# Layer 1's first weights beside layer 0's output, in buffers of their own, and projections ahead of the last output tile

## The chip, the core and the metric

The kernel runs on one core of a Trainium2 chip. The core has five engines that run their own instruction streams and wait for one another through semaphores: TensorE (PE in the profile, PEld for its weight loads), VectorE (DVE), ScalarE (ACT), GpSimd (POOL) and SyncE (SP), which issues most of the transfers between the main memory and the on-chip memory (SBUF). Matmul results go to eight PSUM banks. The metric is the device time of one execution in microseconds (us), lower being better.

## The reference, cut to what matters

Two layers over 1024 latent tokens and 256 context tokens, all in fp32, width 1024. Layer 0 is multi-head latent attention with 16 heads, layer 1 differential attention with 8 heads:

```python
for i in range(2):
    shift, scale, gate = adaln(c, ada_w[i], ada_b[i])           # the context has its own from c_ctx
    h = x * (1.0 + scale[:, None, :]) + shift[:, None, :]
    h_c = ctx * (1.0 + scale_c) + shift_c
    if i == 0: o, o_c = mla_mixer(h, h_c, ...)                  # ends with  o * silu(gate projection)
    else:      o, o_c = diff_mixer(h, h_c, ...)                 # q, k, v, gate = h @ w_in;  o1 - lam_full * o2
    x = layer_norm(DEEPNORM_ALPHA * x + gate[:, None, :] * (o @ out_w[i]), ln_g[i], ln_b[i])
    if i == 0:
        ctx = layer_norm(DEEPNORM_ALPHA * ctx + gate_c * (o_c @ out_w[i]), ln_g[i], ln_b[i])
```

The end of layer 0 is the line with `layer_norm`; its result, scaled and shifted, is the `h` from which layer 1 makes q, k and v. `lam_full` comes from 256 numbers, `diff_lambda`.

## The kernel before, in words

**Precision.** An fp32 matrix product is made of two halves: each operand is split into a high part and a low part (`split`, L175 to L177, for products in a reduced fp32; `split16`, L181 and L182, for fp16 with a scale), and `mm3` (L184 to L187) adds three matmuls: high by high, high by low, low by high. A split is a copy on ScalarE (the high part) and a subtraction on VectorE or GpSimd (the low part).

**Layer 0's output (L853 to L926).** The heads of layer 0 leave their results in `o_d` in main memory. When the last head is done, ten tiles of 128 tokens follow, the two context tiles first (t = 8, 9, 0, 1, ..., 7). Ahead of the first one, two gate rows are loaded. `out_tile` loads a tile of `o_d` and of the gate's silu (`sg_d`), multiplies them on GpSimd (L860), transposes the product on TensorE in two halves (L866, bank "c"), and splits it into `tH` (ScalarE, L176) and `tL` (VectorE, L177). Then TensorE multiplies by the output weights, held in SBUF, in two halves of 512 columns (banks "a" and "b", 24 matmuls each; the records of the three are L185, L186, L187). VectorE evicts each half with the gate and the residual (L877, L878) and takes its statistics (L879, L881); GpSimd raises to the power (L159, L160) and VectorE normalises to `z` (L883). From `z` come two things: the residual of layer 1, written to `zn_d` (VectorE L911, GpSimd L912, a store), and, through eight transposes (L918, bank "d"), layer 1's input `hb` (VectorE L920, GpSimd L922), split into fp16 `h1H` (ScalarE, L925) and `h1L` (GpSimd, L926). The order of instructions on every engine is that of a scheduler in this stage.

**Layer 1's start.** `prod_w(h, which)` makes the weights of one head, `which` being 0 for q and k together and 1 for v and the gate: two loads of 512 KB (L975), a sum of squares on ScalarE (L979), a sum over partitions by a small matmul (L982), an exact power of two as scale (VectorE, GpSimd; L984 to L995, L284 to L287), and two splits into fp16 (L181 on ScalarE, L182 on VectorE). `prod_w(0, 0)` is called behind the tile loop, with its loads on ScalarE's queue and its sum in bank "c". Then the eight PSUM banks become one ring "b" (`set_banks`), the rotary tables and lambda are loaded and lambda computed (L1011 to L1023). `prod_k1`, `prod_q1` and `prod_v1` make K, Q and V of a head. K is made in three chunks (tokens 0 to 511, 512 to 1023, and the 256 of the context), Q in two, each chunk by `proj1` with 24 matmuls, then a rotation (`rope1`, VectorE and GpSimd) and a split whose halves small transfers put in place (`fin`). `prod_w(0, 1)` is woven between K and Q of head 0, `prod_w(1, 0)` between the parts of V. TensorE's order in layer 1 is the order of the text (`manual_schedule`); the other engines' order is the scheduler's.

**Layer 1's gate row** (`gate_row1`, L1208 to L1221) is a vector times matrix made by VectorE with eight loads of 512 KB into the "ws" buffers; its memset, its first load and its first products can be scheduled early, as far as buffers and waits permit.

**Layer 1's output.** During the last head (h = 7), `out_open` closes the pool of the projections and opens one for the output: the rows of `ln_g` and `ln_b`, the buffers `o`, `g`, `tH`, `tL`, `z`, `res`, and the loads and products of out_w's remaining rows (`out_w1`, L1227 and L1229), which the last head's attention runs beside.

**Buffers.** A pool is a stretch of SBUF; `rot` takes the next buffer of a tag from it. A pool opened where an earlier one was closed gives buffers that wait until their memory's earlier user is done. In the kernel before, the pools "a1" and "a1proj" of layer 1 open behind the tile loop, over the memory of the output stage's pool "o0".

Of the kernel before, what the change touches and what calls it, by code (L numbers as in the profile page):

```python
# [9 lines left out]
F32 = mybir.dt.float32  # L10
F32R = mybir.dt.float32r
# [42 lines left out]
def hybrid_kernel(  # L54
# [830 lines left out]

    with ow_ctx, spool("o0") as op0:
# [14 lines left out]
        for t in (8, 9, 0, 1, 2, 3, 4, 5, 6, 7):  # L901
# [12 lines left out]
            hb = op0.tile([P, KT, P], F32, tag="hb", bufs=1, name=nm("hb"))  # L914
            for hh in range(2):
                tb = bank("d")
# [9 lines left out]
            pool.tensor_tensor(h1L[:, :, ts], hb, h1H[:, :, ts], op=ALU.subtract)  # L926

# [3 lines left out]
    TAG1 = {"p0": ([P, NTOK], F32, 2), "p1": ([P, NTOK], F32, 1), "ph": ([P, NT, P], F16, 2),  # L931
# [4 lines left out]
            "ss": ([P, 2], F32, 2), "us": ([P, 1], F32, 3), "es": ([P, 1], F32, 3), "p2s": ([P, 2], F32, 2)}  # L936

    TAGP = {"ws": ([P, 4, 256], F32, 3), "wL": ([P, 4, 256], F16, 4), "wH": ([P, 4, 256], F16, 4),
            "wsq": ([P, D], F32, 1), "sq": ([P, 2], F32, 2), "uw": ([P, 2], F32, 4), "kH": ([P, NTOK], F16, 1), "kL": ([P, NTOK], F16, 1), "gg": ([P, SEQ // P, P], F32, 1),
            "rsw": ([P, 512], F32, 1), "rr": ([P, 512], F32, 1),  # L940
            "kr": ([P, NTOK], F32, 1),
            "Vf": ([P, NT, P], F32, 1), "cosB": ([P, SEQ], F32, 1),
            "sinB": ([P, SEQ], F32, 1)}

    TAGO = {"gb2": ([P, D], F32, 1), "gb3": ([P, D], F32, 1), "o": ([P, D], F32, 3),
            "g": ([P, D], F32, 2), "res": ([P, D], F32, 2), "tH": ([P, KT, P], F32R, 2),
            "tL": ([P, KT, P], F32R, 2), "z": ([P, D], F32, 2), "bs": ([P, 2, 6], F32, 2), "mv": ([P, 4], F32, 2)}
    for k_, v_ in TAG1.items():
        rot(wl, v_[0], v_[1], k_, v_[2], first=True)
# [4 lines left out]
    place = {**{k_: wl for k_ in TAG1}, **{k_: wp for k_ in TAGP}}  # L954
    TAG1.update(TAGP)

    def w1(tag):
        sh, d, b = TAG1[tag]
        return rot(place[tag], sh, d, tag, b)
# [6 lines left out]
    wt, un, us1, es1 = {}, {}, {}, {}  # L966

    def prod_w(h, which, bank_=lambda: bank("b"), load=sp):


        wt[which] = []
        ws, sq = [], w1("sq")
        for q in range(2):
            ws.append(w1("ws"))
            load.dma_start(ws[q], dw[q * 512:(q + 1) * 512, h, which * 256:(which + 1) * 256].rearrange(  # L975
                "(k p) c -> p k c", p=P))
        yield 0
        for q in range(2):
            act.activation(w1("wsq"), ws[q].rearrange("p a b -> p (a b)"), AF.Square, accum_out=sq[:, q:q + 1])  # L979
        yield 0  # L980
        bk = bank_()
        pe.matmul(bk[:, :2], ones, sq, start=True, stop=True)  # L982
        u, p2 = w1("uw"), w1("uw")
        dve.tensor_reduce(u[:, 0:1], bk[:, :2], axis=AX.X, op=ALU.add)  # L984
        pool.tensor_scalar(u[:, 0:1], u[:, 0:1], 1.01, 1e-30, op0=ALU.mult, op1=ALU.add)
        pool.tensor_tensor(u[:, 0:1], u[:, 0:1], poshalf, op=ALU.pow)
        pow2_of(u[:, 1:2], u[:, 0:1], u[:, 0:1], 16384.0, p2)

        dve.tensor_tensor(u[:, 0:1], u[:, 0:1], hun, op=ALU.mult)
        if which:  # L990
            us1[h] = w1("us")
            pool.tensor_tensor(us1[h], u[:, 0:1], vic, op=ALU.mult)
        else:
            es1[h] = w1("es")
            dve.tensor_scalar(es1[h], u[:, 0:1], u[:, 0:1], hic, op0=ALU.mult, op1=ALU.mult)  # L995
        un[which] = u[:, 0:1]
        yield 0
        for q in range(2):
            wH, wL = w1("wH"), w1("wL")
            split16(wH, wL, ws[q], u[:, 1:2])  # L1000
            wt[which] += [(wH[:, j, :], wL[:, j, :]) for j in range(4)]
            yield 0

    for _ in prod_w(0, 0, lambda: bank("c"), act):
        pass
    set_banks(b=8)

    sp.dma_start(cosB, cs1[0])
    sp.dma_start(sinB, cs1[1])
    lamt = w1("rr")[:, :4 * HD]  # L1010
    sp.dma_start(lamt, lam.to_broadcast([P, 4 * HD]))  # L1011
    lt = w1("o1").rearrange("p (a b) -> p a b", a=2)
    ls = w1("sm")
    for j in range(2):
        dve.tensor_tensor(lt[:, j, :], lamt[:, 2 * j * HD:(2 * j + 1) * HD],
                          lamt[:, (2 * j + 1) * HD:(2 * j + 2) * HD], op=ALU.mult)
    dve.tensor_reduce(ls[:, 0:2], lt, axis=AX.X, op=ALU.add)
    act.activation(ls[:, 2:4], ls[:, 0:2], AF.Exp)
    dve.tensor_tensor(nlam, ls[:, 3:4], ls[:, 2:3], op=ALU.subtract)
    dve.tensor_scalar_add(nlam, nlam, -LAMBDA_INIT)  # L1020

    dve.tensor_reduce(lcf[:, 2:3], nlam, axis=AX.X, op=ALU.max, apply_absolute_value=True)
    dve.tensor_scalar_max(lcf[:, 2:3], lcf[:, 2:3], 1.0)  # L1023
    pow2_of(lcf[:, 0:1], lcf[:, 1:2], lcf[:, 2:3], PW, w1("p2s"))
    dve.tensor_tensor(vic, kci, lcf[:, 1:2], op=ALU.mult)

# [455 lines left out]
```

## Time and profile before

| what | us |
| --- | --- |
| median of three runs | 1860.38 |
| lowest and highest run | 1852.12, 1868.84 |
| span of the profiled execution, its own time | 1870.0 |

| stretch of the profiled execution | from | to |
| --- | --- | --- |
| layer 0 up to its last head | 0 | 805 |
| loads of the output stage, until the first transpose | 805.9 | 818.1 |
| ten output tiles on TensorE | 818.1 | 969.4 |
| from the last output matmul to the second K projection | 969.4 | 990.5 |
| layer 1 up to the end | 990.5 | 1870.0 |

The start of a tile is TensorE's first transpose of it (L866): 818.10, 832.78, 846.61, 860.48, 874.63, 894.07, 907.92, 925.73, 939.60, 955.36 for t = 8, 9, 0, ..., 7. In a row of the timeline stand the start, the duration, the engine, the line, the operation and output <- input; in square brackets the idle time ahead of it and what ended it. "xN" means that N instructions in a row are shown as one. A line number is that of the kernel before.

### The profile page before, as it was taken

How to read it: one execution, taken by the hardware profiler on the slowest of the kernel's cores; microseconds unless marked ns; L12 is line 12 of the kernel's file. 1: busy time of each engine (PE TensorE's matmuls, PEld its weight loads, DVE VectorE, ACT ScalarE, POOL GpSimd, SP SyncE). 2: the span in 40 equal slices, each digit the busy share in tenths (PEclk: the TensorE clock that was granted, in tenths of full speed). 3: DMA queues.
4: the chain of work that ended last, by engine and by line, in shares of the span. 5: the costliest groups of instructions: out<-in, count | busy, mean ns of one | idle time of the engine just before them, and what ended most of it. 6: DMA issues, size and time to landing. Idle time of an engine off the chain costs nothing. (4 is left out here: it accounts for less than half of the span.)

```text
span 1870.0 us, 36547 instructions
## 1 busy us (share of the span) xinstructions
PE 1696.2 (91%) x14468; PEld 1237.0 (66%) x14468; DVE 1245.6 (67%) x2072; ACT 1077.1 (58%) x2143; POOL 835.2 (45%) x741
## 2 busy tenths in 40 slices
PE   7889998999999998868979999999999999988998
PEld 3888965656666565556756576767666666666776
DVE  7546766565565657526764777787877777878674
ACT  3432047867777787711123667676767676767542
POOL 1443026767767676646662213222222222433654
PEclk9999799999999999979999999999999999999999
DMA  8245630111111113043333222222121212224341
GB/s 307 62 126 182 189 108 18 39 33 36 42 44 32 32 41 100 25 164 123 124 127 106 71 63 66 62 64 58 56 49 44 59 46 61 63 53 139 99 131 68
DMA packets 111225, 154.84 MB, mean 83 GB/s; under 512 B 13415, under 2 KB 84679, under 8 KB 111054
## 3 DMA queue, kind: packets, MB, share of 16 engines
q1 hardware_dynamic: 104238, 146.22, 26.1%
q10 hardware_dynamic: 6816, 6.29, 1.0%
q8 instruction: 114, 1.87, 0.4%
q14 instruction: 57, 0.47, 0.1%
HBM read 98.65 MB, written 27.07 MB: 67 GB/s over the span
## 5 line engine op out<-in xcount | busy, mean ns | idle before, releaser
L716 POOL TENSOR_TENSOR pl<-p,ph 128x1024 f16<-128x1024 f32 (+1 forms) x176 | 362.8, 2066 | 155.9 <-ACT ph L715 129.5
L1167 ACT ACTIVATE p<-ps_b,mx 128x512 f32<-128x512 f32 (+1 forms) x384 | 230.6, 618 | 83.1 <-DVE mx L1163 82.7
L696 DVE TENSOR_REDUCE mx<-ps_a 128x1 f32<-128x1024 f32 x128 | 155.6, 1223 | 138.2 <-PE ps_a L694 138.2
L714 ACT ACTIVATE p<-ps_a,esc 128x1024 f32<-128x1024 f32 (+1 forms) x176 | 189.2, 1075 | 100.4 <-PE ps_a L772 94.5
L715 ACT CAST ph<-p 128x1024 f16<-128x1024 f32 (+1 forms) x176 | 177.1, 1006 | 5.5
L1161 DVE TENSOR_REDUCE mx<-ps_b 128x1 f32<-128x512 f32 x256 | 165.6, 682 | 0.0
L785 PE MATMUL ps_d<-Vh,pl 128*128 128x65 f16 x1344 | 147.5, 195 | 5.2 <-POOL pl L716 5.1
L782 PE MATMUL ps_d<-Vh,ph 128*128 128x65 f16 x1344 | 149.5, 196 | 0.0
L784 PE MATMUL ps_d<-Vl,ph 128*128 128x64 f16 x1344 | 148.3, 193 | 0.0
L185 PE MATMUL ps_b<-h1H,wH 128*128 128x512 f16 (+1 forms) x384 | 133.5, 348 | 14.1 <-DVE pl L182 6.7
L185 PE MATMUL ps_b<-wH,h1H 128*128 128x256 f16 x512 | 139.5, 272 | 4.4 <-ACT p L1167 4.2
L1192 POOL TENSOR_TENSOR sm<-sm,us 128x1 f32<-128x1 f32 x64 | 18.3, 285 | 271.9 <-DVE sm L1171 258.6
L187 PE MATMUL ps_b<-wH,h1L 128*128 128x256 f16 x512 | 139.5, 273 | 0.0
L186 PE MATMUL ps_b<-wL,h1H 128*128 128x256 f16 x512 | 139.5, 272 | 0.0
L1144 PE MATMUL ps_b<-KS,QS 128*128 128x512 f16 (+1 forms) x384 | 126.1, 345 | 12.0 <-DVE pl L182 6.1
L782 PEld LDWEIGHTS <-ph 128*128 128x128 f16 x1344 | 124.2, 98 | 18.4 <-issue 5.5
L187 PE MATMUL ps_b<-h1H,wL 128*128 128x512 f16 (+1 forms) x384 | 133.2, 347 | 0.8 <-DVE wL L182 0.8
L186 PE MATMUL ps_b<-h1L,wH 128*128 128x512 f16 (+1 forms) x384 | 133.4, 347 | 0.0
L784 PEld LDWEIGHTS <-ph 128*128 128x128 f16 x1344 | 124.9, 99 | 12.4 <-issue 0.8
L770 PE MATMUL ps_a<-qH,KH 100*128 100x512 f16 x320 | 123.6, 386 | 9.7 <-ACT p L714 4.3
L1145 PE MATMUL ps_b<-KS,Q 128*128 128x512 f16 (+1 forms) x384 | 129.1, 345 | 0.0
L785 PEld LDWEIGHTS <-pl 128*128 128x128 f16 x1344 | 124.1, 98 | 6.6 <-POOL pl L716 6.5
(370 smaller groups left out, 5161.9 us busy)
## 6 DMA issues: line engine op xcount, KB each, us to landing
ws<-in_dw SPq DMA_DIRECT2D x30, 512.0 KB, 3.8
adw<-in_ada_w SPq DMA_DIRECT2D x24, 512.0 KB, 5.0
g<-sg_d SPq DMA_DIRECT2D x18, 512.0 KB, 3.7
adaw<-in_ada_w SPq DMA_DIRECT2D x16, 512.0 KB, 7.1
sg_d<-gg ACTq DMA_DIRECT2D x40, 128.0 KB, 2.8
o<-o_d SPq DMA_DIRECT2D x10, 512.0 KB, 3.5
o_d<-op SPq DMA_DIRECT2D x7, 640.0 KB, 3.7
xt<-in_xT SPq DMA_DIRECT2D x16, 256.0 KB, 3.6
```

Of the source, the lines that this page charges most:

```text
L185: pe.matmul(ps, aH, bH, start=start, stop=False, skip_group_check=skip)
L186: pe.matmul(ps, aH, bL, start=False, stop=False, skip_group_check=skip)
L187: pe.matmul(ps, aL, bH, start=False, stop=stop, skip_group_check=skip)
L696: dve.tensor_reduce(mx[:, t, 0:1], ps, axis=AX.X, op=ALU.max)
L714: act.activation(p32[:, :n], st, AF.Exp, scale=esc0)
L715: act.copy(ph[:, :n], p32[:, :n])
L716: pool.tensor_tensor(pl[:, :n], p32[:, :n], ph[:, :n], op=ALU.subtract)
L782: pe.matmul(pv[:, t, :], ph[:, ts], Vh[:, k, h, :], start=(k == kcs[0] and t == 0), stop=False, skip_group_check=True)
L784: pe.matmul(pv[:, t, :V0], ph[:, ts], Vl[:, k, h, :], start=False, stop=False, skip_group_check=True)
L785: pe.matmul(pv[:, t, :], pl[:, ts], Vh[:, k, h, :], start=False, stop=(k == NT - 1), skip_group_check=True)
L1161: dve.tensor_reduce(mx[:, 2 + 2 * m + i:3 + 2 * m + i], b, axis=AX.X, op=ALU.max, negate=True)
L1167: act.activation(p[m][:, c0:c0 + n], b, AF.Exp, bias=nb, accum_out=sm[:, 2 + 3 * m + i:3 + 3 * m + i])
```

## The change

A pool "a1w" for layer 1's weights (raw weights `ws`, split weights `wx` and `wy` with both halves packed in one buffer, squares, scales) is opened ahead of the output stage and stays open to the end. `prod_w`, `proj1` and lambda's computation (`lambda_of`) move ahead of the tile loop, and are called in it: lambda after tile 1, the q and k weights of head 0 after tile 2, the v and gate weights after tile 4. In tile 7 the banks become one ring ahead of the transposes of `z`, TensorE's order becomes that of the text, and K of tokens 0 to 511 comes ahead of those transposes, K of the context and Q of tokens 0 to 511 behind them. Layer 1 then begins with what these three need, and makes the rest of K and Q. In layer 1's output stage `o`, `tH`, `tL` and the row `gb2` use the buffers of "a1w".

```diff
+    TAG1 = {"ws": ([P, D], F32, 3), "wx": ([P, D], F32, 2), "wy": ([P, D], F32, 2), "wsq": ([P, D], F32, 1),
+            "sq": ([P, 2], F32, 2), "uw": ([P, 2], F32, 4), "ls": ([P, 6], F32, 1),
+            "us": ([P, 1], F32, 3), "es": ([P, 1], F32, 3)}
+    wpa = ctx.enter_context(spool("a1w"))
...
+    def prod_w(h, which, bank_=lambda: bank("b"), load=sp):
...
+        for q in range(2):
+            w = w1(("wx", "wy")[q]).bitcast(F16).rearrange("p (a k c) -> p a k c", a=2, k=4)
+            wH, wL = w[:, 0], w[:, 1]
+            split16(wH, wL, ws[q].rearrange("p (k c) -> p k c", k=4), u[:, 1:2])
+            wt[which] += [(wH[:, j, :], wL[:, j, :]) for j in range(4)]
+            yield 0
...
     with ow_ctx, spool("o0") as op0:
...
+            if t == 7:
+                set_banks(b=8)
+                man.enter_context(tc.manual_schedule(engines={ENG["P"]}))
+                kcols, qcols = slice(P, 2 * P), slice(0, P)
+                made = {0: [*proj1(512, 0, kcols)][-1]}
             for hh in range(2):
-                tb = bank("d")
+                tb = bank("d" if t < 7 or t > 7 else "b")
...
             pool.tensor_tensor(h1L[:, :, ts], hb, h1H[:, :, ts], op=ALU.subtract)
+            if t == 7:
+                made[SEQ] = [*proj1(CTX, SEQ, kcols)][-1]
+                made["q"] = [*proj1(512, 0, qcols)][-1]
+                man.close()
+            if t == 1:
+                lambda_of()
+            if t in (2, 4):
+                for _ in prod_w(0, t // 2 - 1, lambda: bank("c"), act):
+                    pass
...
-    for _ in prod_w(0, 0, lambda: bank("c"), act):
-        pass
-    set_banks(b=8)
...
-    def prod_k1(h):
+    def prod_k1(h, made=()):
         kr = w1("kr")
-        for c0, n in CHUNKS:
+        for c0, n in (CHUNKS[0], CHUNKS[2], CHUNKS[1]) if made else CHUNKS:
             c = slice(c0, c0 + n)
-            for ps in proj1(n, c0, slice(P, 2 * P)):
-                yield 3 * n
+            if c0 in made:
+                ps = made[c0]
+            else:
+                for ps in proj1(n, c0, slice(P, 2 * P)):
+                    yield 3 * n
...
-        for tag, src in (("gb2", ln_g), ("gb3", ln_b)):
-            og[tag] = w1(tag)
+        for tag, home, src in (("gb2", "wsq", ln_g), ("gb3", "gb3", ln_b)):
+            og[tag] = w1(home)
...
-        o, g = og[t] = w1("o"), w1("g")
+        o, g = og[t] = w1("ws"), w1("g")
...
-            oT[t] = w1("tH"), w1("tL")
+            oT[t] = [w1(tg).bitcast(F32R).rearrange("p (a b) -> p a b", a=KT) for tg in ("wx", "wy")]
...
-        for _ in chain(weave(chain(prod_k1(0), prod_q1(0, 0), prod_q1(0, 1)), prod_w(0, 1), WAT[0]),
+        for _ in prod_q1(0, 0, made.pop("q")):
+            pass
+        later.pop()()
+        for _ in chain(prod_k1(0, made), prod_q1(0, 1),
                        weave(prod_v1(0), prod_w(1, 0), WAT[1])):
```

150 lines of the change are left out of this document (73 added, 77 removed).

## The prediction

> **What bounds the kernel now.** The page comes first, for the execution's own time, and then the view that cuts the span into stretches: length, then busy time and instructions of TensorE (PE), its weight loads, VectorE (DVE), ScalarE (ACT) and GpSimd (POOL), granted clock, DMA share, GB/s. The four stretches are those that the change touches: the start of layer 0's output stage, its ten token tiles, the handover to layer 1, the preparation of layer 1's output.
>
> ```profile
> span 1870.0 us, 36547 instructions
> ```
> ```profile
> 805.00:818.00 13.00, 0.19 (x4) 0.03 (x1) 0.61 (x2) 0.00 (x0) 2.29 (x1) 0.50 0.73 263
> 818.00:969.00 151.00, 137.73 (x632) 108.90 (x632) 95.54 (x120) 19.96 (x29) 91.89 (x64) 0.96 0.37 123
> 969.00:991.00 22.00, 10.51 (x39) 4.91 (x38) 12.66 (x31) 9.01 (x14) 9.97 (x10) 0.69 0.56 190
> 1712.00:1736.00 24.00, 12.85 (x107) 9.10 (x106) 21.73 (x28) 15.04 (x39) 13.39 (x12) 0.84 0.67 240
> ```
>
> TensorE sets the pace of the tiles (137.7 of 151 us) and stands mostly still in the other three. In the handover it is busy for 10.5 of 22 us, at a mean clock of 0.69. The timeline there, TensorE's rows alone, then GpSimd's, then three of the weight preparation:
>
> ```profile
> 969.00 0.39 PE L187 MATMUL ps_b<-oH,tL 128*128 128x512 f32 x1
> 973.72 1.68 PE L918 MATMUL ps_d<-idr,z 128*128 128x128 f32 x8 [4.34 <-DVE z L883]
> ...
> 981.98 0.61 PE L185 MATMUL ps_b<-h1H,wH 128*128 128x512 f16 x1 [6.36 <-ACT wH L181]
> ...
> 983.80 0.61 PE L187 MATMUL ps_b<-h1H,wL 128*128 128x512 f16 x1 [0.79 <-DVE wL L182]
> ...
> 990.46 0.38 PE L185 MATMUL ps_b<-h1H,wH 128*128 128x512 f16 x1
> ```
> ```profile
> 974.92 2.34 POOL L912 TENSOR_TENSOR res<-res,gb 128x1024 f32<-128x1024 f32 x1 [2.19 <-DVE res L911]
> 977.22 2.04 POOL L922 TENSOR_TENSOR hb<-hb,ab 128x512 f32<-128x512 f32 x2
> ...
> 980.41 2.12 POOL L926 TENSOR_TENSOR h1L<-hb,h1H 128x1024 f16<-128x1024 f32 x1 [0.25 <-ACT h1H L925]
> ```
> ```profile
> 980.78 2.19 ACT L181 ACTIVATE wH<-ws,uw 128x1024 f16<-128x1024 f32 x2 [0.44 <-DVE uw L286]
> ...
> 982.48 2.47 DVE L182 SCALAR_TENSOR_TENSOR wL<-ws,uw,wH 128x1024 f16<-128x1024 f32 x2
> 982.87 1.04 ACT L979 ACTIVATE wsq<-ws 128x1024 f32<-128x1024 f32 x1
> ```
>
> Two waits stand in a row: 4.34 us for the last tile's normalised z, 6.36 us for the weights' high half. The first K projection (24 matmuls) lies between 981.98 and 990.46.
>
> **The change, part by part.** The sum is made against the profiled span of 1870.0 us, 9.6 above the median of the three runs, 1860.38.
>
> *Handover: −14.4 us.* From the end of the last output matmul, 969.39, to 990.46 are 21.1 us. TensorE's work in it is 24 matmuls, at full clock one in 0.215 us (as they follow one another from 990.46 on), 5.2 us, and eight transposes, 1.0 us; so 14.9 us are waits or half clock. After the change the first K projection runs right behind the last output matmul, its weights long made. Then come the transposes (z is there at 973.6, K ends at 974.6), K of the 256 context tokens (24 at half the columns, an estimate of 0.108 us each: 2.6), Q of tokens 0 to 511 (5.2): 14.0 us of work. What follows needs tile 7's h1L, at 982.53 today, 13.1 us after 969.39. Added ahead of it: one product of the layer-1 gate row (L1216 of before) stands on VectorE between L911 and the two hb products, waits for a small load issued at about 971.5 and contends with POOL L912, which ends at 977.26. Worst, hb comes 1.3 us later and h1L at 983.8, 14.4 us: a wait of 0 to 0.5. Gain 14.9 down to 13; I take 14.4. The weights' own work (two scalings of 1.1 on ACT, two low halves of 1.24 on DVE, for each of two weight sets) isn't removed, it moves among the tiles.
>
> The half clock is part of that: at 983.80 a matmul takes 0.61, at 990.46 it takes 0.38. The Trainium skill, "TensorE: Matmul & The Clock Gate", Part 1, "What's actually happening", says that about 3.4 us without work halve the clock until about 3.4 us of work have passed; the rows agree. By it a new wait under that length costs itself only, and one above some 1.7 us more.
>
> *Start: +4 us.*
>
> ```profile
> 805.90 0.36 SPq L798 DMA_DIRECT2D o_d<-op  x1
> 806.36 0.94 SPq L851 DMA_DIRECT2D gate<-gates_d  x2
> ...
> 815.71 2.34 POOL L860 TENSOR_TENSOR o<-o,g 128x1024 f32<-128x1024 f32 x1 [11.96 <-DMA g<-sg_d]
> ```
> ```profile
> DMA to landing us min/median/max: 3.7/3.7/3.7
> ```
>
> The new pool lies below the stage's pool and pushes it over memory that layer 0's last heads still read. The first gate load, today issued right behind the last o_d store, now waits for that store to land: 805.90 + 3.7 = 809.6 instead of 806.36, 3.2 us, and all on SP's queue behind it (second gate row, o, g, res) waits too. POOL L860 waits for g, and TensorE for L860, so nothing hides this. ScalarE also issues three 512 KB weight loads there. At the stretch's 263 GB/s and more, 1.57 MB take up to 6 us of the engines, of which some 3.2 fall in the time that the queue stands. Range 2 (the store is half a usual one) to 7; I take 4, nearest to the 3.2.
>
> *Tiles 3 to 6: +8 us.* This is where I choose. Ten tiles pass in 151 us; where nothing collides one takes 13.85 us (894.07 to 907.92). Tile 4 takes 17.8:
>
> ```profile
> 894.07 1.03 PE L866 MATMUL ps_c<-idr,o 128*128 128x128 f32 x8
> ...
> 907.92 1.03 PE L866 MATMUL ps_c<-idr,o 128*128 128x128 f32 x8
> ...
> 908.85 2.61 DVE L878 SCALAR_TENSOR_TENSOR z<-res,z 128x512 f32<-128x512 f32 x1
> ...
> 914.31 2.85 DVE L883 TENSOR_SCALAR z<-z,mv 128x1024 f32<-128x1024 f32 x1 [0.95 <-POOL mv L160]
> ...
> 925.73 1.03 PE L866 MATMUL ps_c<-idr,o 128*128 128x128 f32 x8
> ...
> 955.36 1.03 PE L866 MATMUL ps_c<-idr,o 128*128 128x128 f32 x8
> ```
> ```profile
> L883 DVE TENSOR_SCALAR z<-z,mv x10: 812/815/2850, 837.3 to 972.8; 128x1024 f32<-128x1024 f32 x10
> ```
>
> L883's median is 0.815 us (last row: least, median and most of ten, in ns); here it and L878 each wait out a GpSimd product that began just before them, the low halves (L177) behind them are late, and TensorE loses 3.9 us. So a shift of half a microsecond decides over some 4. The Trainium skill, "GPSIMD Engine Reference", section 1, says that GpSimd shares its SBUF interfaces with VectorE, which contend when VectorE's instruction reads two SBUF inputs or runs in a two-port mode; these rows agree, and it speaks against this change: the moved L182 reads two. Without contention the next paragraph's 5 us would shrink to some 1.4, and the sum by 3.6.
>
> New in tiles 3 and 5: seven small VectorE operations stand among the two L177, one of them waiting for GpSimd's power, so the second L177 ends some 0.7 us later, GpSimd's L860 goes first and L883 waits behind its 2.34 us. TensorE needs that z for its transposes: 2.5 us each (0 to 4 by tile 4's row), +5. The four L182 come in the same tiles ahead of L877 or L911, which have a bank in reserve.
>
> New on ScalarE: after tile 3's casts come two scalings, h1H of tile 2, the issue of a weight load, a square that waits for its landing, a square of a second load (which SP issues only after the second L182), and only then tile 4's tH, which TensorE needs at once. With tile 3's L866 as zero and tile 4's at 13.85 to 16.4:
>
> ```profile
> DMA to landing us min/median/max: 3.7/3.8/6.7
> ```
>
> L182 ends at 9 to 13 (L883, L911 and the two hb products stand ahead of it), h1H, behind GpSimd's part of hb, at 11 to 17; then 0.5 of issue, 3.8 of landing, two squares of 1.04: tH begins at 18 to 24 instead of 14.5 to 17, a stall of 3.6 to 9.5 us. I take 6 and 1 of half clock. But during it GpSimd and VectorE finish tile 2's and 3's work, so tile 4's own collision (3.9) has no cause any more: +3 net. Tile 6's tH stands behind one more square whose load has landed: 0. Sum +8, from 0 to +20.
>
> *Last head: 0.*
>
> ```profile
> 1734.31 0.79 PE L187 MATMUL ps_b<-oH,tL 128*128 128x512 f32 x1 [7.32 <-DVE tL L177]
> ```
>
> TensorE waits 7.32 us while rows of out_w and ln_g arrive and are multiplied. Four of eleven 512 KB loads now go out before 1712 us, since their buffers are free: at the stretch's rates up to 5 us less. But four L1229 products that wait for loads (each about L182's 1.24) now stand ahead of the attention's splits on VectorE, where three stood ahead of the tL that ends this wait: one product and a late load, up to 3 more. I take 0, with −5 to +3. Lambda and three squares move into tile 8's time, where ScalarE has little to do (20 of the 151 us): 0.
>
> Sum: −14.4 + 4 + 8 + 0 = −2.4; span 1867.6, on the median **1858 us**.
>
> **Rivals.**
>
> *The gain survives.* The start costs 2.5; ScalarE's stall only replaces tile 4's collision, and tiles 3 and 5 lose nothing: −14.4 + 2.5 + 0 = −12: 1848. For it: tile 4 loses its 3.9 us today by a chance of phase, and a stall resets the phase. Against it: ScalarE's order is fixed, and its load can't land before 18.
>
> *The collision of VectorE and GpSimd goes through tiles 3 to 6 (slower).* The four take 13.85 + 17.8 + 29.6 (the last two, 925.73 to 955.36) = 61.3 us. If each goes like tile 4, 71.2, +10, and ScalarE's stall of 6 to 9.5 comes on top: −14.4 + 4 + 10 + 9.5 = +9; with its upper ends (start 7, half clock 3) +15: 1870 to 1875, I say 1872. It decides from a tile-stage cost of 10.4 us on. For it: 92 us of GpSimd and 96 of VectorE already lie in the 151, and some 6 us are added to two tiles. Against it: a stalled TensorE lets both catch up.
>
> *The change doesn't do what it says.* VectorE's gate-row product waits for its load, hb is late, and the second K projection waits 2.5 us for h1L instead of 0.5: 1860 to 1861. Against it: 14.0 us of cover for 13.1.
>
> **How the numbers follow.** Forecast 0.50 (its own range 1852 to 1866), gain survives 0.24, collision 0.18, late h1L 0.08. The signs are mixed, most of the chance is within 1%, which is about what a measurement of this kernel can tell from no change (its runs spread from 1852 to 1869). The first rival reaches down to 1843 (with the last head's −5), the second up to 1878 (with its +3); leaving out the outer parts of both, 2 in 10 together, the range is 1845 to 1875. Faster than 1841.8 needs the first rival with the last head's gain: 0.07. Slower than 1879 needs the collision with a bad last head: 0.12. Within: 0.81.
>
> **What would show it.** Right: the first gate load issued near 809.6; TensorE's first output transpose 3 to 6 us later; tile 4's tH on ScalarE behind two squares that wait for a weight load; L883 above 2 us in tiles 3 and 5; between last output matmul and the second K projection about 14 us at full clock, without the two waits. Wrong: a tile stage as long as today's, a wait for h1L of several microseconds, or a last head that moves by more than 5 us.

## The result, and the profile after

| | before | after |
| --- | --- | --- |
| median of 14 runs each, us | 1864.87 | 1872.76 |
| lowest and highest run | 1852.12, 1868.86 | 1867.08, 1877.30 |
| span of the profiled execution | 1870.0 | 1870.4 |

The ratio of the times, after to before, is 1.0046, with a 95% interval of 1.0033 to 1.0059: the changed kernel is 0.46% slower, some 8.6 us (6 to 11) on the 1862 us around which the medians of the kernel before lay from one comparison to the next. That is within 1% and inside the range, but it is a loss, where the forecast was a gain of 2.4.

The spans of the two profiled executions differ by 0.4 us only. Cut into stages they differ much more. Each bound of this table but the last is a row of TensorE: the end of the last value matmul of layer 0, the first output transpose (L866), the end of the last output matmul, the first scores of head 0, the ten transposes of attention's last block (1719.08 before), and the first low-half matmul of layer 1's output (L187, 1734.31 before). The rest goes up to the issue of the last store.

| stage, us | before | after | difference |
| --- | --- | --- | --- |
| layer 0, to its last value matmul | 805.2 | 794.4 | −10.8 |
| start of the output stage | 12.9 | 17.6 | +4.7 |
| ten output tiles | 151.3 | 165.8 | +14.5 |
| handover, to the first scores of head 0 | 63.3 | 48.3 | −15.0 |
| layer 1 from there to attention's last block | 686.4 | 687.3 | +0.9 |
| last block and first output matmuls of layer 1 | 15.2 | 20.7 | +5.4 |
| the rest | 133.1 | 133.7 | +0.6 |

The change touches all rows but the first. They sum to +11.1 us; that layer 0 ends 10.8 us earlier in the profile is a matter of its own (the last experiment).

The stretches of the changed kernel, columns as in the prediction: start, tiles, TensorE's 14 us behind the last output matmul, and the last block of layer 1.

```profile
794.40:812.00 17.60, 0.00 (x1) 0.01 (x1) 0.61 (x2) 0.00 (x0) 2.34 (x1) 0.50 0.82 283
812.00:977.75 165.75, 143.42 (x637) 112.77 (x638) 105.44 (x149) 31.40 (x46) 96.07 (x68) 0.92 0.38 128
977.75:991.75 14.00, 14.00 (x81) 7.96 (x80) 7.24 (x12) 1.12 (x2) 9.53 (x8) 1.00 0.36 114
...
1712.00:1736.00 24.00, 11.14 (x66) 8.17 (x67) 23.63 (x22) 11.91 (x29) 21.19 (x12) 0.72 0.40 148
```

The handover is as it was meant to be: in 14.00 us TensorE is busy for 14.00, at full clock, where it had two waits and half clock. The timeline there, VectorE's and GpSimd's row of interest:

```profile
983.11 1.28 DVE L1237 SCALAR_TENSOR_TENSOR gate<-ws,sc,gate 128x1024 f32<-128x1024 f32 x1
...
989.77 2.13 POOL L1007 TENSOR_TENSOR h1L<-hb,h1H 128x1024 f16<-128x1024 f32 x1 [1.16 <-ACT h1H L1006]
```

The gate row's product is there, and h1L of tile 7 is done at 991.90, as TensorE ends what doesn't need it at 991.75. The other three stretches pay for it. TensorE's clock over the tiles fell from 0.96 to 0.92, and in the last stretch from 0.84 to 0.72, with VectorE at 23.6 of 24 us and GpSimd at 21.2 instead of 13.4.

**Start.** The timeline of the changed kernel, queues and engines together:

```profile
794.88 1.02 ACTq L907 DMA_DIRECT2D ws<-in_dw  x2
795.08 0.36 SPq L798 DMA_DIRECT2D o_d<-op  x1
801.15 0.81 SPq L851 DMA_DIRECT2D gate<-gates_d  x2
...
812.00 0.48 PE L866 MATMUL ps_c<-idr,o 128*128 128x128 f32 x1 [17.62 <-POOL o L860]
```

The first gate load is issued 6.1 us behind the store, as the prediction had it in kind: it waits for the store to land (5.9 us after its issue), and ScalarE's queue moves weights meanwhile.

**Tiles.** The timeline of the changed kernel, engine by engine: TensorE's waits in tiles 9, 4 and 6; then ScalarE ahead of tile 4; then VectorE and GpSimd.

```profile
829.99 0.49 PE L185 MATMUL ps_a<-oH,tH 128*128 128x512 f32 x1 [1.94 <-ACT tH L176]
...
904.37 1.04 PE L866 MATMUL ps_c<-idr,o 128*128 128x128 f32 x8
915.24 0.80 PE L185 MATMUL ps_a<-oH,tH 128*128 128x512 f32 x1 [9.83 <-ACT tH L176]
...
948.72 0.79 PE L185 MATMUL ps_a<-oH,tH 128*128 128x512 f32 x1 [2.98 <-ACT tH L176]
```
```profile
905.17 1.04 ACT L1006 CAST h1H<-hb 128x1024 f16<-128x1024 f32 x1 [9.31 <-POOL hb L1003]
905.23 0.37 ACTq L907 DMA_DIRECT2D ws<-in_dw  x1
912.38 1.06 ACT L911 ACTIVATE wsq<-ws 128x1024 f32<-128x1024 f32 x1 [6.17 <-DMA ws<-in_dw]
...
913.56 1.06 ACT L911 ACTIVATE wsq<-ws 128x1024 f32<-128x1024 f32 x1
...
914.62 1.06 ACT L176 CAST tH<-ps_c 128x512 fp32r<-128x512 f32 x2
```
```profile
894.55 0.81 DVE L883 TENSOR_SCALAR z<-z,mv 128x1024 f32<-128x1024 f32 x1 [0.26 <-POOL mv L160]
...
899.81 2.44 DVE L182 SCALAR_TENSOR_TENSOR wx<-ws,uw,wx 128x1024 f16<-128x1024 f32 x1
902.17 2.06 DVE L182 SCALAR_TENSOR_TENSOR wy<-ws,uw,wy 128x1024 f16<-128x1024 f32 x1
```

Tile 4 (from 904.37 to 930.15, 25.8 us) shows the mechanism in one chain, read backwards: TensorE waits 9.83 us for tH; tH stands on ScalarE behind two squares; the first square waits for a weight load; that load was issued behind h1H; and h1H waited until 905.17 for GpSimd's part of hb. ScalarE runs its instructions in order, so a cast whose own input had been there since 905.4 began at 914.62. The load itself ended ScalarE's wait only 7.1 us after its issue, 912.38 against 905.23; SyncE had issued three other transfers of 512 KB between 904.26 and 905.43. The matmuls after this wait run at half clock: the first is 0.80 us long instead of some 0.4, and the mean clock of the tile is 0.80. Tiles 9 and 6 have the same wait in small, 1.94 and 2.98 us, also behind squares.

A part of the loss is in no wait. At full clock the matmuls of the tiles follow one another every 0.2335 us on average, 0.2283 in the kernel before; tile 0, which nothing disturbs, takes 14.05 us instead of 13.87. Over 480 matmuls that is some 2.5 of the 14.5 us. It is so in every kernel that has the weights' pool ahead of the output stage, and in none of those that have not (b_out_only and e_l0tail have 0.2284). Its cause was not tried.

**Last block of layer 1.** TensorE's rows, then VectorE's, of the changed kernel:

```profile
1724.83 0.29 PE L1211 MATMUL ps_b<-vh,pl 128*128 128x128 f16 x1 [5.29 <-DVE pl L182]
...
1734.00 0.80 PE L187 MATMUL ps_b<-oH,wy 128*128 128x512 f32 x1 [3.83 <-DVE wy L177]
```
```profile
1718.39 2.37 DVE L1250 SCALAR_TENSOR_TENSOR res<-res,gsub,gate 128x1024 f32<-128x1024 f32 x1
1720.68 3.36 DVE L1250 SCALAR_TENSOR_TENSOR z<-z,gsub,gate 128x1024 f32<-128x1024 f32 x1
...
1724.04 0.74 DVE L182 SCALAR_TENSOR_TENSOR pl<-ps_b,lcf,ph 128x512 f16<-128x512 f32 x1
```

The one wait of 7.32 us became two, 5.29 and 3.83. Two products of out_w's rows, 2.37 and 3.36 us long beside GpSimd's subtractions (one at 1731.18 in the kernel before took 1.27), now stand on VectorE ahead of `pl`, the probabilities' low half for which TensorE waits. Before, they stood behind it.

### The profile page after: what moved, and what is told of

It is laid out like the page before. It is cut to its first block, busy times and chain, and to the rows that moved or that the text cites. A ratio compares the mean times of both kernels' runs of the same rounds, so it can differ in the third digit from the quotient of the medians.

```text
span 1870.4 us, 36537 instructions
## 1 busy us (share of the span) xinstructions
PE 1694.9 (91%) x14468; PEld 1238.4 (66%) x14468; DVE 1245.0 (67%) x2072; ACT 1077.6 (58%) x2143; POOL 841.6 (45%) x741
## 5 line engine op out<-in xcount | busy, mean ns | idle before, releaser
L182 DVE SCALAR_TENSOR_TENSOR pl<-ps_b,lcf,ph 128x512 f16<-128x512 f32 (+1 forms) x192 | 117.4, 654 | 15.8 <-ACT ph L181 15.8
L181 ACT ACTIVATE ph<-ps_b,lcf 128x512 f16<-128x512 f32 (+1 forms) x192 | 115.2, 648 | 19.3 <-PE ps_b L1201 19.3
L1201 PE MATMUL ps_b<-idr,p 128*128 128x128 f32 x640 | 103.5, 278 | 24.3 <-ACT p L1188 16.4
L771 PE MATMUL ps_a<-qH,KL 96*128 96x512 f16 x320 | 121.8, 381 | 0.0
L772 PE MATMUL ps_a<-qL,KH 96*128 96x512 f16 x320 | 121.2, 379 | 0.0
L1211 PE MATMUL ps_b<-vh,pl 128*128 128x128 f16 x640 | 111.3, 220 | 5.3 <-DVE pl L182 5.3
```

Of the source, the lines that this page charges most:

```text
L182: dve.scalar_tensor_tensor(lo, src, scale, hi, op0=ALU.mult, op1=ALU.subtract)
```

## The experiments

My theory after the result: four places, each with its own cause, pay for the handover: the start (weight loads and the wait for the store), ScalarE's order in tiles 9, 4 and 6, the contention in tiles 3 and 5 (0.7 us each), and the order on VectorE in the last block. The rivals: the tiles are lost to contention of VectorE and GpSimd alone; the start is lost to the wait for the store alone; the last block is lost to GpSimd's subtractions. Unless said otherwise, an edit is on the changed kernel, and a ratio is against the kernel before.

### e_pin: the late weight loads out of ScalarE's way

```diff
-            ws.append(w1("ws"))
+            ws.append(spare() if spare and q else w1("ws"))
+            if h == 1 and which == 0:
+                pool.tensor_copy(ws[q][:, :1], h1L[:, 0, SEQ - 1:SEQ])
```

The fourth load gets a buffer of its own (`spare`), so that it needn't wait for L182, and the loads of head 1 wait for tile 7.

> Edit on the changed kernel: the fourth load of head 0's weights gets a buffer of its own, so it is issued at the start of the output stage, and the loads of head 1's weights are held back until tile 7's h1L is there (two one-column copies on GpSimd). No square on ScalarE waits for a load between tile 3 and tile 7 any more; all computation stays. Theory A (ScalarE's casts blocked behind squares that wait for loads cost tile 4 its 8.0 us and most of tile 6's 3.1): tile 4's period falls from 25.8 to 14 to 18 us, the 9.83 us wait for tH is gone, the whole is 8 to 11 us faster than the changed kernel, about 0.1% to 0.2% faster than before. Rival B (the moved weight scalings contend with GpSimd, and the block only moves that loss): tile 4 keeps 20 us or more, or tiles 5 to 7 take over what it gives back, and the whole gains less than 4 us.

Ratio 1.0018 (1.0007 to 1.0029). The 9.83 us are gone; tile 4 falls from 25.8 to 20.7 and tile 6 from 18.9 to 15.5. TensorE's waits in tile 4 of this kernel:

```profile
910.04 0.50 PE L185 MATMUL ps_a<-oH,tH 128*128 128x512 f32 x1 [1.37 <-ACT tH L176]
912.92 0.50 PE L187 MATMUL ps_a<-oH,tL 128*128 128x512 f32 x1 [1.68 <-DVE tL L177]
918.10 1.94 PE L1001 MATMUL ps_d<-idr,z 128*128 128x128 f32 x8 [2.33 <-DVE z L883]
```

So ScalarE's order made the stall, but of 9.83 us only 5.1 came back: with the stall gone, the collision of L883 with a GpSimd product is back as a wait of 2.33 us, and a wait for tL beside it. The stall had covered it. Tile 9 grew from 15.2 to 17.3. By the runs the edit gained some 5 us, less than the 8 to 11 of theory A, and tile 4 kept the 20 us of the rival.

### e_sp: the same loads on SyncE's queue

```diff
-                for _ in prod_w(0, t // 2 - 1, lambda: bank("c"), act):
+                for _ in prod_w(0, t // 2 - 1, lambda: bank("c"), sp):
```

> Edit on the changed kernel: the four loads of head 0's weights go out on SyncE's queue, behind the first tile's loads, instead of ScalarE's at the start. With the store's landing taken out of the way (the padded kernel) the start fell only from 17.6 to 15.7 us (12.9 before). Theory A (the rest, 2.8 us, is three 512 KB loads sharing the transfers' bandwidth with the first tile's): from the last value matmul to the first output transpose 14.5 to 16 us, the first gate load still waiting for the store. Theory B (the store's landing alone is late, 6 us instead of 3.7, because of something else): the start stays at 17 us or more. Tile 4 changes little (its square still stands behind a load): the whole 1 to 4 us faster than the changed kernel.

Ratio 0.9994 (0.9974 to 1.0014): no difference from before, and 0.5% better than the changed kernel. Start of this kernel, SyncE's queue and TensorE:

```profile
794.93 0.36 SPq L798 DMA_DIRECT2D o_d<-op  x1
797.35 0.81 SPq L851 DMA_DIRECT2D gate<-gates_d  x2
...
808.15 1.97 PE L866 MATMUL ps_c<-idr,o 128*128 128x128 f32 x8 [13.92 <-POOL o L860]
```

SyncE issues the three weight loads from 815.19 on, behind the start. From the store to the first gate load there are 2.4 us instead of 6.1; from the gate load to the first transpose 10.8 in both. So the start (13.9 us instead of 17.6) loses 3.7 of its 4.7 us through the weight loads, and they act on the store: it lands 5.9 us after its issue beside 1.57 MB of weights, 2.3 here, and the gate row waits for it. The wait behind an undisturbed store costs 1. Tile 4 fell to 19.2 too, against the expectation: a load that isn't issued by ScalarE needn't wait there behind h1H. Tile 6 stayed (19.0).

### e_pad: without the wait for the store

```diff
     with ow_ctx, spool("o0") as op0:
+        op0.tile([P, 2 * D], F32, tag="pad", bufs=1, name="pad")
```

> Edit on the changed kernel: 8 KB per partition left unused at the bottom of the output stage's pool, so that the gate rows no longer lie over the buffer from which the last head's results are stored. Theory A (the first gate load waits for that store to land, and all of SP's queue with it): the gate loads follow the store within 1 us, and from the store's issue to the first output transpose it takes 12 to 13.5 us instead of 16.9; 3 to 4.5 us faster than the changed kernel. Rival B (the three weight loads on ScalarE's queue take the transfers' bandwidth at the start): the gate loads are issued early, but the first transpose still comes 15 us or more after the store.

Ratio 1.0072 (1.0052 to 1.0091), slower still. The 8 KB move the gate rows off the memory that the store reads, and the load goes out at once:

```profile
799.06 0.36 SPq L798 DMA_DIRECT2D o_d<-op  x1
799.51 1.52 SPq L851 DMA_DIRECT2D gate<-gates_d  x2
```

Yet the start only fell from 17.6 to 15.7. Now the loads for tile 8 run beside the weights, and from gate load to first transpose it is 14.5 us instead of 10.8: the delay through the weight loads moves from the store to what comes in its place. This kernel also lost 4.2 us in the handover (52.5), where TensorE has a new wait of 2.35 us for `rr`, a tile of the rotation that ScalarE writes, and 2 in the tiles. Why the padding brings these was not traced.

### e_noproj: weights early, projections not ahead

```diff
-            if t == 7:
-                set_banks(b=8)
-                man.enter_context(tc.manual_schedule(engines={ENG["P"]}))
-                kcols, qcols = slice(P, 2 * P), slice(0, P)
-                made = {0: [*proj1(512, 0, kcols)][-1]}
...
-            if t == 7:
-                made[SEQ] = [*proj1(CTX, SEQ, kcols)][-1]
-                made["q"] = [*proj1(512, 0, qcols)][-1]
-                man.close()
```

> Edit on the changed kernel: the weights are still made among the tiles, but no projection stands ahead of tile 7's transposes, and K and Q come in the order of before. It parts the handover's gain (63.3 us before, 48.3 after, from the last output matmul to the first scores) in two. Theory: the weights' 6.36 us wait is gone, the 4.34 us wait for z comes back, and K of tokens 512 to 1023 waits for h1L some 2 us: 54 to 57 us, so about half the gain from each half of the change; the whole 6 to 9 us slower than the changed kernel. Rival (early weights are all of it, the projections could as well stand behind the transposes): 48 to 51 us.

Ratio 1.0102 (1.0072 to 1.0132). The handover is 56.1 us: early weights alone save 7.2 of the 15.0, the reordered projections 7.8. TensorE's two waits that remain in this kernel:

```profile
982.62 1.94 PE L994 MATMUL ps_d<-idr,z 128*128 128x128 f32 x8 [4.34 <-DVE z L883]
992.48 0.38 PE L186 MATMUL ps_b<-h1L,wx 128*128 128x512 f16 x1 [0.89 <-POOL h1L L1002]
```

The 4.34 us for z are word for word the wait of before; the 6.36 for the weights are gone.

### b_out_only: the buffers alone, on the kernel before

```diff
+    TAGW = {"ws": ([P, D], F32, 3), "wx": ([P, D], F32, 2), "wy": ([P, D], F32, 2), "wsq": ([P, D], F32, 1),
+            "sq": ([P, 2], F32, 2), "uw": ([P, 2], F32, 4)}
+    wpa = ctx.enter_context(spool("a1w"))
...
-        o, g = og[t] = w1("o"), w1("g")
+        o, g = og[t] = w1("ws"), w1("g")
...
-            oT[t] = w1("tH"), w1("tL")
+            oT[t] = [w1(tg).bitcast(F32R).rearrange("p (a b) -> p a b", a=KT) for tg in ("wx", "wy")]
```

The weights' buffers stand behind the tile loop, in a pool of their own, and layer 1's output takes its o, tH, tL and ln_g row from them; nothing is made earlier.

> Edit on the kernel before: only the buffers are changed. Layer 1's weights get a pool of their own behind the tile loop, and layer 1's output stage takes o, tH, tL and gb2 from it, as in the change; no weight is made early and no projection moves. Theory A (the last head's 6.2 us come from these buffers alone: out_w's rows land earlier, and VectorE's four products and GpSimd's four splits stand in each other's way ahead of the attention's low half): 5 to 7 us slower than before (0.3% to 0.4%), with a wait of TensorE for pl near 5 us about 11 us after the last head's 1280-column transposes begin. Rival B (the loss in the last head is a matter of phase, brought by the earlier stages): within 2 us of before, and the wait looks like that of before, 7.3 us for tL alone.

Ratio 1.0079 (1.0063 to 1.0094). Its last block takes 20.7 us, as in the changed kernel, with the same wait:

```profile
1735.17 0.79 PE L187 MATMUL ps_b<-oH,wy 128*128 128x512 f32 x1 [3.83 <-DVE wy L177]
```

So the 5.4 us of the last block come from where the output's buffers lie, not from the early weights. (Its handover is 7.5 us longer than that of before, 70.8: the new buffers delay weights and squares there by an 11.7 us wait. The changed kernel doesn't have that.)

### e_outlate: the same buffers, the loads held back

```diff
+            if tag == "gb2":
+                gl = w1("z")
+                pool.memset(gl[:, :1], 0.0)
+                pool.tensor_copy(og[tag][:, :1], gl[:, :1])
...
+        if t < 2:
+            pool.memset(g[:, :1], 0.0)
+            pool.tensor_copy(o[:, :1], g[:, :1])
```

Four one-column operations make the ln_g row and the first two loads of o wait until the output's own pool is free, as they had to before.

> Edit on the changed kernel: four one-column GpSimd operations make the loads of ln_g's row and of the first two o tiles wait for buffers of layer 1's output pool, as they did before the change; 11 loads of 512 KB stand again in the last head, and VectorE's order there is again that of before (the attention's three low halves ahead of out_w's products). Theory A (the earlier loads let VectorE's products go first, so that the attention's pl and tL wait): 15 to 16 us from the last head's transposes to the output stage's first low-half matmul instead of 20.7, the whole 4 to 6 us faster than the changed kernel, within 0.25% of before. Rival B (the buffers themselves, by where they lie or by whom they wait for, cost the time): 19 us or more.

Ratio 1.0020 (1.0002 to 1.0037). The last block is back at 15.3 us, with the one wait of before to the hundredth:

```profile
1729.49 0.80 PE L187 MATMUL ps_b<-oH,wy 128*128 128x512 f32 x1 [7.32 <-DVE wy L177]
```

Loading earlier was the loss: what landed earlier let the scheduler put products of out_w ahead of what TensorE waits for.

### e_dvelo: GpSimd relieved in the last block

```diff
-        split(oHL[k][0], oHL[k][1], ws, e_lo=pool)
+        split(oHL[k][0], oHL[k][1], ws, e_lo=pool if k < NOW else dve)
```

> Edit on the changed kernel: the low halves of the last four out_w rows are subtracted on VectorE instead of GpSimd. Theory A (the two engines exclude each other: a product of 1.28 us took 2.4 to 3.4 us beside GpSimd's 2.35 us splits): VectorE's products go back to 1.3 us, the shared time falls from 4 x 3.6 to 4 x 2.5 us, TensorE's waits in the last head fall from 10 to about 6 us, 3 to 5 us faster than the changed kernel. Rival B (VectorE's queue is the cause, four products stand ahead of pl whatever GpSimd does): four more operations of 1.2 us on that queue make pl later, TensorE's wait grows by up to 4 us.

Ratio 1.0051 (1.0034 to 1.0069), as the changed kernel. The last block stays at 20.9 us; the wait has only moved into one piece:

```profile
1733.11 0.29 PE L1211 MATMUL ps_b<-vh,pl 128*128 128x128 f16 x1 [9.79 <-DVE pl L182]
```

With GpSimd idle, VectorE's next three products take 1.27 to 1.28 us, so GpSimd's subtractions did lengthen them to 2.37, 3.36 and 2.64. But the four subtractions now stand on VectorE ahead of `pl` (2.97 us and three times 1.22), and the wait is no shorter; what follows the block is 2.6 us shorter. So this run doesn't part the rival from the order on VectorE. e_outlate does as far as it goes: there GpSimd keeps its subtractions, and with the old order the loss is gone.

### v2 and v3: the cures together

v2 has e_pin's buffer and pin, e_sp's queue, e_outlate's late loads, and in the output stage's pool the buffers `hb` and the first `z` ahead of the gate rows:

```diff
     with ow_ctx, spool("o0") as op0:
+        hb0 = op0.tile([P, KT, P], F32, tag="hb", bufs=1, name=nm("hb"))
+        z0 = op0.tile([P, D], F32, tag="z", bufs=2, name=nm("z"))
         gate = [op0.tile([P, D], F32, tag=f"gate0{s}", bufs=1, name=f"gate0{s}") for s in range(2)]
```

> Edit on the changed kernel: all the cures together. Head 0's loads on SyncE's queue, the fourth into a buffer of its own, head 1's loads held back until tile 7, the first buffers of the output stage's pool (over the stored results) given to z and hb, and the late loads of the last head. By the stages measured so far: start 13 to 14 us (12.9 before), tiles 154 to 160 (151.3), handover 48 to 49 (63.3), last head as before: 4 to 12 us faster than before, a ratio of 0.994 to 0.998. If the collision of VectorE and GpSimd in tile 4 stays at its 20.7 us and tile 9 at 17, only 4; if a hidden cost remains, no faster than before.

Ratio 0.9922 (0.9896 to 0.9948), median 1850.93: faster than both kernels, 14 us under the one before. Stretches of v2: start, tiles, and the 14 us behind the last output matmul.

```profile
798.06:811.25 13.19, 0.00 (x0) 0.00 (x0) 0.61 (x2) 0.00 (x0) 2.34 (x1) 0.51 0.77 258
811.25:966.18 154.93, 140.05 (x637) 109.15 (x638) 104.58 (x149) 29.16 (x42) 97.03 (x68) 0.96 0.40 134
966.18:980.18 14.00, 14.00 (x82) 8.01 (x81) 6.12 (x11) 1.04 (x1) 8.99 (x10) 1.00 0.34 114
```

Start and last block (13.2 and 15.6 us) are those of before, the tiles 3.6 us longer instead of 14.5, the handover is kept (48.0).

v3 is v2 with e_dvelo's edit.

> Edit on the kernel with all the cures (ratio 0.992 to before): the low halves of the last four out_w rows on VectorE instead of GpSimd. On the changed kernel that left the wait at 20.9 us and took 2.6 us off what follows. With the order of before on VectorE: from the last head's transposes to the first low-half matmul 15 to 17 us, the rest 131 instead of 132.5, so 0 to 3 us faster than the kernel with all the cures, ratio 0.990 to 0.993; if the four operations delay tL, no gain.

Ratio 0.9973 (0.9952 to 0.9995), so worse than v2: with the loads late again, four more subtractions on VectorE make the last block 18.3 us instead of 15.6. (The tiles are 1.6 us longer too, for which the edit gives no reason.)

### before_again: the kernel before, profiled once more

No edit. Layer 0 ended 7 to 11 us later in the profile of before than in every kernel with another layout of SBUF, though the order of instructions up to there is the same on all five engines; I held that profile for an odd one.

> The kernel before, unchanged, profiled once more. In nine profiles of kernels with the same layer 0 its last value matmul ended between 794.2 and 798.4 us, in the first profile of before at 805.2. Theory: that profile was a slow execution in layer 0, of which the changed kernel has no part: the last value matmul ends between 794 and 799 us, the span is 1859 to 1864 us, and the stages behind it stand as in the first profile within 1 us (start 12.9, tiles 151.3, handover 63.3, last head 15.2). Rival: the change of SBUF's layout makes layer 0 faster by 8 us: 803 to 806 us again.

That fell: layer 0 ended at 803.4 us in the second profile also (805.2 in the first, 794.2 to 798.4 in the changed layouts). The span was 1868.2; the ratio to the kernel before, the same code, run beside it, 0.9984 (0.9963 to 1.0005).

### e_l0tail: one block of layer 0's last head 1.5 us later

On the kernel before, with its layout:

```diff
         act.copy(ph[:, :n], p32[:, :n])
+        units.append(n)
+        if len(units) == 153:
+            act.copy(ph[:, :n], p32[:, :n])
```

> On the kernel before, with its memory layout untouched: ScalarE makes the high half ph of one softmax block of layer 0's last head twice (the block behind the fourth row of out_w), so that GpSimd's pl of that block starts some 1.5 us later; nothing else is changed and nothing is left out. Layer 0's tail took 805.2 and 803.4 us in the two profiles of the kernel before, 794.2 to 798.4 in all kernels with the changed layout. What differs first between them: the fourth row of out_w lands 0.6 to 1.4 us later in the changed layout, ScalarE's queue behind it is late by as much, and GpSimd's pl of that block starts behind VectorE's product L808 of the row (732.27, 1.28 us) instead of ahead of it (734.94, 2.97 us). Theory of the race: the delay alone, without the layout, gives the same: the row's product takes 1.3 us, the end of layer 0's last value matmul comes at 794 to 799 us, and the kernel is 0.994 to 0.997 of before. Rival: the layout or the later rows' landings decide for themselves; then the row's product may be short, but the stretch from that row to the last value matmul stays as long, its end is at 803 to 806 us, and the ratio is 1.000 to 1.001.

VectorE and GpSimd at the fourth row of out_w, in the kernel before, and then in this one (where the lines are 5 higher):

```profile
734.70 4.22 POOL L716 TENSOR_TENSOR pl<-p,ph 128x1024 f16<-128x1024 f32 x2 [1.65 <-ACT ph L715]
734.94 2.97 DVE L808 SCALAR_TENSOR_TENSOR oL<-ows,usc,oH 128x1024 fp32r<-128x1024 f32 x1
```
```profile
731.45 1.28 DVE L813 SCALAR_TENSOR_TENSOR oL<-ows,usc,oH 128x1024 fp32r<-128x1024 f32 x1
733.63 3.25 POOL L721 TENSOR_TENSOR pl<-p,ph 128x1024 f16<-128x1024 f32 x2 [4.08 <-ACT ph L720]
```

This race turns as expected: GpSimd begins behind VectorE's product, not 0.24 us ahead of it, and the product takes 1.28 us instead of 2.97. From the context's values (`op`, L794 of before, at 739.16, and at 736.91 here) to the last value matmul it is 66.0 us before, 66.1 in before_again, 57.7 in the changed kernel (at most 58.4 in e_pin, e_pad, e_sp, v2 and v3), and 59.5 here. Layer 0 ended at 796.4 us, the span was 1861.4. But that the race at the fourth row makes the difference is not shown, and one profile speaks against it. In e_outlate, whose tail takes 57.5 us, it goes as in the kernel before:

```profile
733.61 4.22 POOL L716 TENSOR_TENSOR pl<-p,ph 128x1024 f16<-128x1024 f32 x2 [1.71 <-ACT ph L715]
733.80 3.02 DVE L808 SCALAR_TENSOR_TENSOR oL<-ows,usc,oH 128x1024 fp32r<-128x1024 f32 x1
```

What all the short tails have in common lies later: the product of the sixth row takes 1.27 or 1.28 us in them, and 2.98 in both profiles of the kernel before. No run moves that one alone. And the ratio is 1.0002 (0.9986 to 1.0018), which is the rival's number: a gain in the profile of 8.6 us that the timed runs don't have.

The profile and the timed runs go together if most timed executions of the kernel before already end layer 0 early, and the profiled ones don't. (If so, the early end in one profile of e_l0tail need not come from its delay.) The second profile's execution took 1870.3 us, the highest of that kernel's eight runs, whose median was 1861.1; the first one's span is above the highest of the 14 runs. A sum over all kernels points the same way. "Stages" is the sum of the stages without layer 0, against the first profile of before; "runs" is the ratio, less one, times 1862 us.

| kernel | stages, us | runs, us (95%) |
| --- | --- | --- |
| after | +11.1 | +8.6 (6 to 11) |
| e_pin | +4.3 | +3.4 (1 to 5) |
| e_pad | +14.8 | +13.4 (10 to 17) |
| b_out_only | +12.7 | +14.7 (12 to 18) |
| e_dvelo | +9.3 | +9.5 (6 to 13) |
| e_sp | −1.4 | −1.1 (−5 to +3) |
| e_outlate | +5.0 | +3.7 (0 to 7) |
| e_noproj | +17.1 | +19.0 (13 to 25) |
| v2 | −11.3 | −14.5 (−19 to −10) |
| v3 | −6.3 | −5.0 (−9 to −1) |
| e_l0tail | +0.2 | +0.4 (−3 to +3) |

Layer 0 left out, the traces give the runs within some 3 us in every row; with its 7 to 11 us taken in, none but v2's fits. This is inferred, since no profile of an execution of before with an early layer 0 was had. What makes the tail short in the other layouts stays open.

## Why the prediction was wrong

By its own terms, in us of the profile:

| term | predicted | measured |
| --- | --- | --- |
| handover | −14.4 | −15.0 |
| start | +4 (2 to 7) | +4.7 |
| tiles | +8 (0 to 20) | +14.5 |
| last head | 0 (−5 to +3) | +5.4 |
| elsewhere | 0 | +1.5 |
| sum | −2.4 | +11.1 |

**Handover: right**, in mechanism and size. K, its context chunk and Q cover 14.0 us, and the wait for h1L (ready at 991.9) is not there. The gate row's product did come in between, as priced, without harm.

**Start: right in size, only half right in cause.** The prediction added up the store's landing at 3.7 us and some of the loads' bandwidth. But the 3.7 are those of the earlier stores of 640 KB; this one has 256 KB and lands after 2.3 us where nothing is beside it (e_sp), after 5.9 beside the loads. So the two are one: without the loads the wait is worth 1 us.

**Tiles: the term that failed first.** Its mechanism, ScalarE's in-order queue in tile 4, is what the trace shows; its size was not. Predicted for tile 4: 6 of stall, 1 of half clock, less the 3.9 of its own collision, +3. Measured: 9.83 of stall, just above the upper bound of 9.5; 2.1 of half clock (25.78 less 13.85 and 9.83), since some dozen matmuls ran at 0.43 us instead of 0.23; less the 3.96 that tile 4 lost before: +8.0.

The term that was mis-sized is the landing of the weight load. Counted from tile 3's first transpose (889.82), h1H began at 15.4, inside the predicted 11 to 17; the load then took 7.1 us to end ScalarE's wait, where the prediction had 0.5 of issue and 3.8 of landing, a median over the kernel; so tH began at 24.8 and not at 18 to 24. With 4.3 us instead of 7.1 the stall would have come to some 7, an estimate. L182 was late too: it ended at 14.4, predicted 9 to 13. The cover that the prediction claimed for the collision was real: L883 is late again, but TensorE doesn't wait for it, and e_pin brought the wait back. I chose 6 within 3.6 to 9.5 although the chain, L182 beside GpSimd and h1H behind GpSimd's hb, was known to be contended; the trace had L182 at 2.44 and 2.06 us, not 1.24.

Tile 6 at 0 was wrong: +3.1, a square and an h1H ahead of tH, for the same reason. Nor does a shorter wait always cost itself only, as the prediction had it: tile 6, with 2.98 us of waiting, ran at a mean clock of 0.82, while tile 4 of e_sp, with waits of 2.44 and 2.35, ran at 1.00. Tile 9 at 0 was wrong too: lambda and three squares, called hidden because ScalarE is busy for 20 of 151 us, stood in line ahead of a tH that TensorE wanted (1.94). And no term stood for matmuls that follow one another more slowly, some 2.5 us over the ten tiles.

The opposite error was in tiles 3 and 5: 2.5 each predicted, 0.7 each measured, as L883 won the race there (0.81 us at 894.55). That is the 1.4 in all that the prediction gave for the case without contention, and not because there is none: the Trainium skill, "GPSIMD Engine Reference", section 1, has VectorE and GpSimd contend for their SBUF interfaces, and the two L182 at 2.44 and 2.06, with L1250 up to 3.36, agree.

**Last head: the term that failed second.** It weighed an earlier arrival of rows (−5) against products on VectorE ahead of what TensorE needs (+3), and took the middle. b_out_only and e_outlate show the second to be what counted, at nearly twice its bound: products of 2.37 and 3.36 us instead of 1.24, and TensorE's clock at 0.50 from 1724 to 1734.

**The rivals.** "The collision goes through tiles 3 to 6" gave +9 to +15, for 23.5 to 29.5 us lost in start, tiles and half clock; the measured +8.6 came out near its lower end, but by luck and not by that mechanism: tiles 3 and 5 hardly collided, and the stall and its like on ScalarE, with the last block, made the sum. "The gain survives" failed at ScalarE's order, which the prediction itself named against it. "Late h1L" did not occur.

**The base.** The sum was made against a profile 9.6 us above the median, and the prediction passed that on as an offset. It looks to have been layer 0 in that execution, which is inferred and not shown.

## What to carry to other kernels

Work moved off a stalled stretch is paid where it lands: look there at the in-order queue of every engine that it uses, and above all for an instruction that waits for a transfer ahead of one that TensorE needs; busy shares (ScalarE 13%) say nothing about it. An earlier load is not free either: it takes bandwidth from those beside it, and it lets a scheduler put its consumer ahead of more urgent work. Once the places had been found by experiment, most of the loss had a cheap cure (a spare buffer, another queue, a load held back), and with them the moved work gained 0.8%; the tiles kept 3.6 us, of which the slower matmuls are some 2.5.

## What was not expected of the hardware

Some tenths of a microsecond decide what a VectorE instruction costs beside GpSimd. A product of 128x1024 with two operands in SBUF took 1.28 us where GpSimd began behind it (732.27 in the changed kernel, GpSimd at 733.30) and 2.97 where it began 0.24 us behind GpSimd (734.94 in the kernel before). The Trainium skill, "SBUF — State Buffer", "SBUF: two separate sides", says that of the two engines, where VectorE's instruction has two SBUF inputs, the one that starts first holds the shared ports for its whole instruction, while the other stands still; L808 at 734.94 ends 1.1 us after GpSimd's first `pl` (734.70 with half of 4.22, to 736.8), which agrees. Layer 0's tail, which is full of such races, took some 8 us less in the profiles of all ten kernels with another layout of SBUF than in the two of the kernel before, without a change in any engine's order; which race makes this, and whether the layout does, is not shown.

Three transfers of 512 KB on ScalarE's queue made one store on SyncE's queue land 3.6 us later, 5.9 us after its issue instead of 2.3. The Trainium skill, "DMA: Bandwidth & Descriptors", "Issuing engines are not separate DMA queues", says that transfers interleave on the same DMA engines whichever engine starts them; e_sp, where the same loads go out later and the store lands after 2.3 us, agrees.
